# Rotary embedding: the adds of nine tiles on the TensorE, and transfers of 2 MB

## The chip, the cores and the metric

The kernel runs on one core of a Trainium2 chip. The metric is the device time of one execution in microseconds, the median over several runs. A profile is one execution seen by the hardware profiler; its times count from the start of its span.

## The reference

```python
def reference(x, cos, sin):          # x: (8, 2048, 8, 64), cos and sin: (2048, 32), all float32
    x1 = x[..., : x.shape[-1] // 2]
    x2 = x[..., x.shape[-1] // 2 :]
    cos = cos[None, :, None, :]
    sin = sin[None, :, None, :]
    out1 = x1 * cos - x2 * sin
    out2 = x1 * sin + x2 * cos
    return np.concatenate([out1, out2], axis=-1)
```

Every head of 64 numbers is split in two halves of 32. Each output half is one input half times the cosine plus or minus the other half times the sine. The input and the output hold 33.55 MB each, and every byte is read once and written once.

## The kernel before

The sequence of 2048 positions is laid over the 128 partitions, 16 neighbouring positions to a partition. A tile holds four of these 16 for one batch entry: 128 partitions of 2048 floats, which is 1 MB in rows of 8 KB. There are four blocks of positions and eight batch entries, so 32 tiles; the loop runs over the blocks outside and the batch inside.

The two tables are small (0.26 MB each). SBUF holds them in `sin_sb` and `cos_sb`. VectorE builds `ssin` from the sine table (line 58 with the sign turned, line 59 as it is), and copies the cosine table into PSUM as `cos_ps` (line 60). The helper `rep` repeats a table along the heads by an access pattern of step 0, so no repeated table is stored.

The work of a tile is this. GpSimd multiplies the swapped halves of `xt` by `ssin` into `t2`, in two instructions (line 73), one for each half. VectorE multiplies `xt` by `cos_ps` into `t1` in PSUM (line 78), and then adds `t1` and `t2` back into `xt` (line 83). ScalarE issues the store of `xt` (line 84) and computes nothing. All loads of x are issued by SP (line 55), those of the tables by ScalarE (lines 48 and 49).

The buffers are: 20 slots of `xt`, which is 160 KB of each partition, three slots of `t2` in SBUF, and one slot of `t1` in PSUM. The first 20 loads need nothing but a slot; each later load waits for the store of the tile 20 places earlier. The kernel writes no order and no semaphores by hand: the tile framework orders the instructions of each engine and inserts the waits. No engine but VectorE and GpSimd does arithmetic.

Of the kernel before, what the change touches and what calls it, by code (L numbers as in the profile page):

```python
# [2 lines left out]

# [4 lines left out]


@with_exitstack  # L10
def kernel(
    ctx: ExitStack,
    tc: tile.TileContext,
    x: bass.AP,
    cos: bass.AP,
    sin: bass.AP,
    out: bass.AP,
):
    nc = tc.nc
    f32 = mybir.dt.float32  # L20

    B, S, H, D = x.shape
    Dh = D // 2
    P = 128
    HD = H * D
    R = S // P

    SL = 4
    n_blk = R // SL
    FREE = SL * HD  # L30

    xv = x.rearrange("b (q r) h d -> b q (r h d)", q=P)
    ov = out.rearrange("b (q r) h d -> b q (r h d)", q=P)
    cos_src = cos.rearrange("(q r) d -> q r d", q=P)
    sin_src = sin.rearrange("(q r) d -> q r d", q=P)

    const_pool = ctx.enter_context(tc.tile_pool(name="const", bufs=1))
    cps_pool = ctx.enter_context(tc.tile_pool(name="cps", bufs=1, space=bass.MemoryType.PSUM))
    t1_pool = ctx.enter_context(tc.tile_pool(name="t1p", bufs=1, space=bass.MemoryType.PSUM))
    xpool = ctx.enter_context(tc.tile_pool(name="xpool", bufs=20))  # L40
    t2_pool = ctx.enter_context(tc.tile_pool(name="t2p", bufs=3))

    cos_sb = const_pool.tile([P, R, Dh], f32, tag="cb")
    sin_sb = const_pool.tile([P, R, Dh], f32, tag="sb")
    ssin = const_pool.tile([P, R, 2, Dh], f32, tag="ss")
    cos_ps = cps_pool.tile([P, R, Dh], f32, tag="cp")

    nc.scalar.dma_start(out=sin_sb, in_=sin_src)
    nc.scalar.dma_start(out=cos_sb, in_=cos_src)

    tiles = [(b, l) for l in range(n_blk) for b in range(B)]
    xts = []
    for i, (b, l) in enumerate(tiles):
        xt = xpool.tile([P, FREE], f32, tag="xt", name=f"xt{i}")
        nc.sync.dma_start(out=xt, in_=xv[b, :, l * FREE : (l + 1) * FREE])
        xts.append(xt)

    nc.vector.tensor_scalar_mul(ssin[:, :, 0, :], sin_sb, -1.0)  # L58
    nc.vector.tensor_copy(ssin[:, :, 1, :], sin_sb)  # L59
    nc.vector.tensor_copy(cos_ps, cos_sb)  # L60

    def rep(a, n):
        return dataclasses.replace(a, ap=[a.ap[0][:], a.ap[1][:], [0, n], a.ap[-1][:]])

    for i, (b, l) in enumerate(tiles):
        xt = xts[i]
        t1 = t1_pool.tile([P, FREE], f32, tag="t1")
        t2 = t2_pool.tile([P, FREE], f32, tag="t2")

        for u in range(2):  # L70
            dst = t2.rearrange("p (rh u d) -> p rh u d", u=2, d=Dh)[:, :, u, :]
            src = xt.rearrange("p (rh u d) -> p rh u d", u=2, d=Dh)[:, :, 1 - u, :]
            nc.gpsimd.tensor_mul(  # L73
                out=dst.rearrange("p (r h) d -> p r h d", h=H),
                in0=src.rearrange("p (r h) d -> p r h d", h=H),
                in1=rep(ssin[:, l * SL : (l + 1) * SL, u, :], H),
            )
        nc.vector.tensor_mul(  # L78
            out=t1.rearrange("p (r k d) -> p r k d", r=SL, d=Dh),
            in0=xt.rearrange("p (r k d) -> p r k d", r=SL, d=Dh),  # L80
            in1=rep(cos_ps[:, l * SL : (l + 1) * SL, :], 2 * H),
        )
        nc.vector.tensor_add(out=xt, in0=t1, in1=t2)  # L83
        nc.scalar.dma_start(out=ov[b, :, l * FREE : (l + 1) * FREE], in_=xt)


# [1 line left out]
_INS = ['x', 'cos', 'sin']  # L88
_OUTS = [((8, 2048, 8, 64), 'float32')]


# [23 lines left out]
```

## Time and profile before

| | |
|---|---|
| time, median of 8 runs | 168.3 us (168.0 to 168.43) |
| the profiled execution | 168.31 us, of which its span is 166.5 us |
| VectorE busy | 148.2 us, 89% of the span |
| GpSimd busy | 146.3 us, 88% of the span |
| bytes moved | 67.65 MB, on average 406 GB/s over the span |
| loads of x by SP | 32, 1024 KB each, 20.8 us from issue to landing |
| stores by ScalarE | 32, 1024 KB each, 10.8 us from issue to landing |

In the profile DVE is VectorE, POOL is GpSimd, ACT is ScalarE, PE is TensorE and SP is SyncE, which issues loads only; a "q" behind a name means the engine's own queue of issues. A digit in a row of slices is the busy share of one fortieth of the span in tenths. In a line of a group stand the line of the code, the engine, the operation, output and inputs, their shapes and the number of instructions; after the first bar the busy time and the mean duration in ns, and after the second the idle time ahead of the group with what ended it.

### The profile page before, as it was taken

To read this page: it belongs to the slowest core of one execution; us is meant where nothing else is said; L and a number is where in the kernel's file an instruction comes from. 1 tells how busy PE (TensorE), PEld (TensorE's weight loads), DVE (VectorE), ACT (ScalarE), POOL (GpSimd) and SP (SyncE) were. 2 spreads that over 40 slices of the span, in tenths; PEclk is the share of its full clock that TensorE was granted. 3 is DMA by queue.
4 is the path that set the end of the run, shared out by engine and by line. 5 is a ranking of instruction groups with operands and counts; after the bars stand their busy time and mean duration, and the time that the engine had idled before them with its cause. 6 is when DMAs were issued, how large, how long until landed. Compare 5 with 4: busy or idle time off the path is not lost.

```text
span 166.5 us, 381 instructions
## 1 busy us (share of the span) xinstructions
DVE 148.2 (89%) x67; POOL 146.3 (88%) x68
## 2 busy tenths in 40 slices
DVE  0169999999999999999999999999999999999980
POOL 0299999999999999999999999999999999998000
DMA  5999999999999999999999999999999999999656
GB/s 181 427 428 419 378 431 425 425 433 427 427 427 427 427 423 433 425 431 423 425 425 429 425 431 427 427 423 433 429 423 427 429 425 427 429 431 425 272 220 252
DMA packets 9506, 67.65 MB, mean 406 GB/s; under 512 B 1056, under 2 KB 1056, under 8 KB 1312
## 3 DMA queue, kind: packets, MB, share of 16 engines
q10 hardware_dynamic: 4896, 34.08, 48.6%
q1 hardware_dynamic: 4608, 33.56, 48.3%
q14 instruction: 2, 0.02, 0.0%
HBM read 34.08 MB, written 33.55 MB: 406 GB/s over the span
## 4 chain that ended last, share of the span: by engine, by line
POOL 50%; DVE 29%; issue 14%; DMA 4%; DVEq 0%
POOL t L73 50%; DVE xt L83 15%; DVE t L78 14%; DMA sin_sb<-in_sin_dram 4%; DVE ssin L58 0%; DVEq L83 0%
## 5 line engine op out<-in xcount | busy, mean ns | idle before, releaser
L73 POOL TENSOR_TENSOR t<-xt,ssin 128x1024 f32<-128x1024 f32 x64 | 146.1, 2319 | 6.8 <-DVE ssin L58 6.8
L83 DVE TENSOR_TENSOR xt<-t,t 128x2048 f32<-128x2048 f32 x32 | 73.3, 2291 | 3.3
L78 DVE TENSOR_TENSOR t<-xt,cos_ps 128x2048 f32<-128x2048 f32 x32 | 73.5, 2296 | 1.1
L58 DVE TENSOR_SCALAR ssin<-sin_sb 128x512 f32<-128x512 f32 x1 | 0.4, 428 | 6.7 <-DMA sin_sb<-in_sin_dram 6.7
L60 DVE COPY cos_ps<-cos_sb 128x512 f32<-128x512 f32 x1 | 0.7, 695 | 2.4 <-DMA cos_sb<-in_cos_dram 2.4
L59 DVE COPY ssin<-sin_sb 128x512 f32<-128x512 f32 x1 | 0.4, 420 | 0.0
L99 POOL MEMSET const-float32-0.0<- 128x1 f32 x1 | 0.1, 100 | 0.2 <-issue 0.2
L99 POOL MEMSET const-bfloat16-1.0<- 128x1 bf16 x1 | 0.1, 103 | 0.0
L99 POOL MEMSET const-uint8-127<- 128x1 uint8 x1 | 0.1, 103 | 0.0
L99 POOL MEMSET const-float32-1.0<- 128x1 f32 x1 | 0.1, 100 | 0.0
## 6 DMA issues: line engine op xcount, KB each, us to landing
xt<-in_x_dram SPq DMA_DIRECT2D x32, 1024.0 KB, 20.8
out_dram<-xt ACTq DMA_DIRECT2D x32, 1024.0 KB, 10.8
sin_sb<-in_sin_dram ACTq DMA_DIRECT2D x1, 256.0 KB, 5.9
cos_sb<-in_cos_dram ACTq DMA_DIRECT2D x1, 256.0 KB, 8.7
```

The lines of the kernel that those rows point to most:

```text
L58: nc.vector.tensor_scalar_mul(ssin[:, :, 0, :], sin_sb, -1.0)
L59: nc.vector.tensor_copy(ssin[:, :, 1, :], sin_sb)
L60: nc.vector.tensor_copy(cos_ps, cos_sb)
L73: nc.gpsimd.tensor_mul(out=dst.rearrange("p (r h) d -> p r h d", h=H), in0=src.rearrange("p (r h) d -> p r h d", h=H), in1=rep(ssin[:, l * ...
L78: nc.vector.tensor_mul(out=t1.rearrange("p (r k d) -> p r k d", r=SL, d=Dh), in0=xt.rearrange("p (r k d) -> p r k d", r=SL, d=Dh), in1=rep ...
L83: nc.vector.tensor_add(out=xt, in0=t1, in1=t2)
L99: nc = _bacc.Bacc("TRN2", target_bir_lowering=False, num_devices=1)
```

## The change

A pair of tiles now shares one slot `xt`, loaded and stored as 2 MB with rows of 16 KB. Only the first pair is loaded in two halves, and only the last is stored in two. There are nine slots of a pair. The tables' loads move from ScalarE's queue to the head of SP's.

The tiles are of three kinds. An "A" tile is computed as before. A "B" tile leaves its add out of VectorE: VectorE writes `t1` to SBUF (pool `t1s`, three slots), and TensorE multiplies 512 columns of `t1` and of `t2` by an identity matrix, both into the same PSUM bank, so that the bank holds their sum; ScalarE copies the bank to `xt`. A "C" tile leaves GpSimd out too: VectorE multiplies `xt` by the sine into a second `t1s` slot, and TensorE adds that with the halves swapped, with the negative identity where the sign is minus. The kinds stand in a dictionary: tiles 5, 13 and 21 are C, the two tiles behind each are B, the other 23 are A. (The change's short name speaks of ten tiles, and of four C; the last of its steps sets the three groups that the code has.)

The diff, cut to what computes:

```diff
-    xpool = ctx.enter_context(tc.tile_pool(name="xpool", bufs=20))
+    o_pool = ctx.enter_context(tc.tile_pool(name="op", bufs=2, space=PSUM))
+    xpool = ctx.enter_context(tc.tile_pool(name="xpool", bufs=9))
+    t1s_pool = ctx.enter_context(tc.tile_pool(name="t1s", bufs=3))
     t2_pool = ctx.enter_context(tc.tile_pool(name="t2p", bufs=3))
...
-    nc.scalar.dma_start(out=sin_sb, in_=sin_src)
-    nc.scalar.dma_start(out=cos_sb, in_=cos_src)
+    nc.sync.dma_start(out=sin_sb, in_=sin_src)
+    nc.sync.dma_start(out=cos_sb, in_=cos_src)
...
+    for i, (b, l) in enumerate(pairs):
+        xt = xpool.tile([P, PAIR], f32, tag="xt", name=f"xt{i}")
+        for lo, n in [(0, FREE), (FREE, FREE)] if i == 0 else [(0, PAIR)]:
+            nc.sync.dma_start(
+                out=xt[:, lo : lo + n],
+                in_=xv[b, :, l * PAIR + lo : l * PAIR + lo + n],
+            )
...
+    nc.gpsimd.memset(eye, 0.0)
+    nc.gpsimd.affine_select(out=eye, in_=eye,
...
+    nc.scalar.copy(sin_ps, sin_sb)
+    nc.scalar.mul(neye, eye, -1.0)
...
+    kinds = {}
+    for g in (5, 13, 21):
+        kinds |= {g: "C", g + 1: "B", g + 2: "B"}
...
+        if kind == "C":
+            t2 = t1s_pool.tile([P, FREE], f32, tag="t1s", name="t2c")
+        else:
+            t2 = t2_pool.tile([P, FREE], f32, tag="t2")
+        if kind == "A":
+            t1 = t1_pool.tile([P, FREE], f32, tag="t1")
+        else:
+            t1 = t1s_pool.tile([P, FREE], f32, tag="t1s")
...
+        if kind == "C":
+            nc.vector.tensor_mul(
+                out=t2.rearrange("p (r k d) -> p r k d", r=SL, d=Dh),
+                in0=xk,
+                in1=rep(sin_ps[:, r0 : r0 + SL, :], 2 * H),
             )
+        else:
+            for u in range(2):
+                nc.gpsimd.tensor_mul(
...
         nc.vector.tensor_mul(
             out=t1.rearrange("p (r k d) -> p r k d", r=SL, d=Dh),
...
+        if kind == "A":
+            nc.vector.tensor_add(out=xt, in0=t1, in1=t2)
+        elif kind == "B":
+            for j in range(FREE // C):
+                o = o_pool.tile([P, C], f32, tag="o")
+                cs = slice(j * C, (j + 1) * C)
+                nc.tensor.matmul(o, eye, t1[:, cs], start=True, stop=False)
+                nc.tensor.matmul(o, eye, t2[:, cs], start=False, stop=True)
+                nc.scalar.copy(xt[:, cs], o)
+        else:
+            G = C // Dh
+            for u in range(2):
+                for j in range(FREE // 2 // C):
+                    o = o_pool.tile([P, C], f32, tag="o")
+                    gs = slice(j * G, (j + 1) * G)
+                    nc.tensor.matmul(o, eye, t1u[:, gs, u, :], start=True, stop=False)
+                    nc.tensor.matmul(
+                        o, eye if u else neye, t2u[:, gs, 1 - u, :], start=False, stop=True
+                    )
+                    nc.scalar.copy(xu[:, gs, u, :], o.rearrange("p (g d) -> p g d", d=Dh))
...
+        if i == n_tiles - 2:
+            nc.scalar.dma_start(out=ov[b, :, base : base + FREE], in_=xt)
+        elif i == n_tiles - 1:
+            nc.scalar.dma_start(out=ov[b, :, base + FREE : base + PAIR], in_=xt)
+        elif half:
+            nc.scalar.dma_start(out=ov[b, :, base : base + PAIR], in_=pt)
```

## The prediction, made before the changed kernel ran

> **What bounds the kernel now.** I read the page from the top: busy shares, then the 40 slices.
>
> ```profile
> DVE 148.2 (89%) x67; POOL 146.3 (88%) x68
> ...
> DVE  0169999999999999999999999999999999999980
> POOL 0299999999999999999999999999999999998000
> DMA  5999999999999999999999999999999999999656
> GB/s 181 427 428 419 378 431 425 425 433 427 427 427 427 427 423 433 425 431 423 425 425 429 425 431 427 427 423 433 429 423 427 429 425 427 429 431 425 272 220 252
> ```
>
> Three things are full at once. VectorE and GpSimd read 9 from slice 4 on, and the DMA engines move about 427 GB/s from slice 2 to slice 37. Only the last three slices fall to 220 to 272. So there are two nearly equal bounds, and the ends decide which is first. The groups by line give the unit prices:
>
> ```profile
> L73 POOL TENSOR_TENSOR t<-xt,ssin 128x1024 f32<-128x1024 f32 x64 | 146.1, 2319 | 6.8 <-DVE ssin L58 6.8
> L83 DVE TENSOR_TENSOR xt<-t,t 128x2048 f32<-128x2048 f32 x32 | 73.3, 2291 | 3.3
> L78 DVE TENSOR_TENSOR t<-xt,cos_ps 128x2048 f32<-128x2048 f32 x32 | 73.5, 2296 | 1.1
> ```
>
> A tile costs GpSimd 146.1/32 = 4.57 us. VectorE starts a tile every 4.73 us: in the chain below its multiply starts at 152.36 and again at 157.08.
>
> ```profile
> 152.36 2.31 DVE t L78
> ...
> 157.08 2.31 DVE t L78
> ...
> 159.48 2.29 DVE xt L83
> ```
>
> The chain ends in VectorE's last add, at 161.8; the last store follows and the span ends at 166.5, 4.7 us later. The windows show what the transfers did meanwhile:
>
> ```profile
> core 0: us, DVE busy (x) POOL busy (x), PEclk, DMA share, GB/s
> ...
> 156.50:166.50 10.00, 5.14 (x3) 0.00 (x0) 1.00 0.52 213
> 24.00:154.00 130.00, 126.23 (x56) 129.30 (x57) 1.00 1.01 427
> ```
>
> For 130 us the transfers run at a share of 1.01. Only when their backlog is gone do they wait for VectorE: from 156.5 on they move 2.13 MB, which at 427 GB/s takes 5.0 us. With the 1.4 us after the last packet (the slices of transfers in this window end near 165.1) the end would be 156.5 + 5.0 + 1.4 = 162.9. **So a faster VectorE is worth at most 3.6 us; then the transfers are the end.** At the front, the timeline shows:
>
> ```profile
> 7.21 9.27 POOL L73 TENSOR_TENSOR t<-xt,ssin 128x1024 f32<-128x1024 f32 x4 [6.76 <-DVE ssin L58]
> 9.87 0.69 DVE L60 COPY cos_ps<-cos_sb 128x512 f32<-128x512 f32 x1 [2.41 <-DMA cos_sb<-in_cos_dram]
> 10.60 2.30 DVE L78 TENSOR_TENSOR t<-xt,cos_ps 128x2048 f32<-128x2048 f32 x1
> 13.00 2.29 DVE L83 TENSOR_TENSOR xt<-t,t 128x2048 f32<-128x2048 f32 x1
> ```
>
> GpSimd waits for the sine table until 7.2, VectorE for the cosine table until 9.9; the tables share the engines with x.
>
> **What the Trainium skill says.** "FP8 and Floating Point Precision", TensorE Precision Notes: true FP32 takes four passes through the array. "TensorE: Matmul & The Clock Gate", Back-to-back issue gap: N/1.2 ns per matmul cold, N/2.4 + 2.5 ns warm; its Part 1 says that the clock starts at half and rises after some 3.4 us of sustained work. The trace of before has no matmul, so neither is confirmed. "GPSIMD Engine Reference", 1. Specifications: GpSimd contends with VectorE instructions with two SBUF inputs. Here every VectorE operation on a tile has one PSUM input (`cos_ps` or `t1`), GpSimd is at 129.3 of 130 us, and the change keeps that form (`sin_ps`, `cos_ps`), so I keep 4.57 us.
>
> **The change part by part.**
>
> *Tables first, on SP.* 0.52 MB of tables, then 1.05 MB of x in one queue. The tables' 2 KB packets took 84 ns (85 of them are 11.2% of 16 engines in the window from 1 to 5 us), so they need 1.4 us; the first packets move at about 1.7, half a pair takes 2.5 us, and some 0.8 us passes until it has landed: 6.4. GpSimd starts near 6.5 (0.7 earlier), VectorE's first multiply too, and its first add follows GpSimd at 6.5 + 4.6 = 11.1 against 13.0. Gain 1.9 us of VectorE. The identity and its negative are made meanwhile by engines that are idle until 6.5: cost nothing; a bound of 1 us if GpSimd's select is slow. SP issues 19 DMAs instead of 32 and ScalarE 17 instead of 34, at 0.33 us each; neither queue was what the transfers waited for.
>
> *2 MB transfers.* A packet of 8 KB took 309 ns (588 packets with 523 of data, 101.4% of ten us of 16 engines), one of 2 KB 84 ns: a fixed 9 ns and 27.3 GB/s. A 16 KB packet would take 609 ns where two take 618: 1.5% of 158 us, 2.3 us. The other bound is nothing, if rows are cut. I take half, 1.1 us: the floor is 161.8. Nine slots of 2 MB hold 18 MB against 20; the first store waits for two tiles, but loads fill that time.
>
> *VectorE.* The code marks nine tiles, not the ten of the change's title. Six "B" lose the add (6 x 2.36 = 14.2 us); three "C" have two multiplies, as dear as before (2.291 and 2.296 us to SBUF and to PSUM show that the target is free). *GpSimd* loses three tiles: 3 x 4.57 = 13.7 us.
>
> *TensorE and ScalarE.* Each of the nine tiles needs eight matmuls of 512 columns. Four passes at 2.4 GHz make 0.86 us each, at 1.2 GHz 1.71 us (both from the pages' prices). With about 4 us of cold start a group of three takes 8.9 + 6.9 + 6.9 = 22.7 us; cold throughout 41. The four evacuations of a tile by ScalarE cost 186 + 0.833 x 512 = 0.61 us each by "ScalarE: Activation LUTs", What ACT_TABLE_LOAD costs; two output banks cover that behind 1.7 us of matmuls.
>
> *The waits that come in.* First, the second B of a group takes a `t1s` slot that C holds until its last matmul. Queued behind it on VectorE are all later A tiles. Second, each B keeps its `t2` until TensorE has read it, so GpSimd has one of three slots meanwhile. Walk a group, from VectorE's start of tile 5 at 31.7. C's multiplies end at 36.4, TensorE works C until 45.4, B 6 until 52.3, B 7 until 59.2. B 6's multiply ends at 38.8. The order of VectorE's stream is left to the tile framework, which can put ready work of tile 8 ahead of the blocked B 7; nothing in the trace of before shows such a choice. **I take it that it does so.** Then tile 8 is multiplied at 38.8, added by 45.4 (GpSimd has it at 43.1), B 7 is multiplied until 47.8, tile 9 ends at 52.4 (GpSimd 45.4 to 50.0, having waited 2.3), tile 10 at 59.2 (GpSimd 52.3 to 56.9, again 2.3), 11 at 63.9, 12 at 68.6. Eight tiles take 36.9 us against 37.8 before. The last add: 31.7 + 3 x 36.9 + 3 x 4.73 = 156.6, the store to 161.3. ScalarE issues the stores and waits in its stream for TensorE; those of pairs 2 and 3 come late, while loads have slots to fill the engines.
>
> *Sum.* Compute ends at 161.3, the transfers at 161.8; I add 0.7 for gaps at the hand-over from loads to stores: span 162.5. The profiled execution took 168.31 for a span of 166.5, 1.8 around it, and lies on the median of 168.3. **Forecast 164.3 us**, 2.4% less.
>
> **The rivals.**
>
> *1. TensorE becomes the bound through the slots (slower).* If VectorE's stream stays in program order, B 7's multiply stands from 38.8 to 45.4 with everything behind it. Tile 8 then ends at 52.6, tile 9 waits for GpSimd, which got its slot at 52.3, until 59.3, tile 10 (slot at 59.2) until 66.2, 12 until 75.7: 44.0 us a group, that is 21.3 plus TensorE's 22.7. The end is 31.7 + 132 + 14.2 + 4.7 = 182.6, so 184.4 us. It is slower once TensorE needs over 17.3 us a group (31.7 + 3p + 14.2 + 4.7 = 166.5 gives p = 38.6), 0.72 us a matmul. For it: three slots and four passes. Against it: work of tile 8 is ready. A stream partly in that order gives values between, from 169.
>
> *2. The clock stays low.* 13.7 us a tile, 41.1 a group. With reordering TensorE sets the period: near 175 us; in program order near 239. For it: TensorE is idle between groups. Against it: a group is longer than the rise takes.
>
> *3. The transfers lose what the engines gain.* Large transfers on nine slots leave a gap while stores wait for a group; 4 to 5 us of it bring 167.5 to 169. Against it: by 97 us, the end of the second group, full engines have moved 95.5 us x 427 GB/s = 40.8 MB, some nineteen transfers of a pair; with seven pairs stored twelve are loaded, and sixteen (nine slots and the seven set free) could be.
>
> *4. Faster matmuls or none of these waits:* compute ends near 157, and the transfers alone set 160.5 to 162.9: 162.3 to 164.7.
>
> **How the numbers follow.** My forecast with rival 4 has 0.58, its own range 162.4 to 167.5; rival 1 0.22 (169 to 186); rival 2 0.12; rival 3 0.08, half of it within 0.2% of before, which is about what a measurement of this kernel can tell from no change. Faster: 0.58 + 0.02 = 0.60. Same: 0.05. Slower: 0.35. The range of 162.4 to 182 leaves out the upper half of rival 1, most of it on the 239 side of rival 2, and 0.03 below.
>
> **What the profile would show.** Right: DMA near 427 to 433 GB/s until the last slices, the last add near 157, matmul groups of about 22 us, VectorE near 138 us and GpSimd near 133 us busy. The first add near 11. Rival 1: VectorE's line of the `t1s` multiply waiting some 6.6 us for TensorE three times, and GpSimd waiting for TensorE. Rival 2: matmuls of 1.7 us throughout. Rival 3: slices of DMA under 8 with VectorE busy. A compute end after 158 would make the forecast wrong.

## The result, and the profile after

The changed kernel takes **177.04 us** (median of 11 runs, 175.84 to 177.92) against 168.29 us in runs of the kernel before beside it: a ratio of 1.052, with a 95% interval of 1.0504 to 1.0536. The forecast was 164.3 us, and the chance given to slower was 0.35. The time lies inside the range, but it moved the other way. The profiled execution has a span of 175.0 us. A run more than 1.5% above the fastest of its kernel counts as slow; every ratio here compares fast runs alone, and only the first run with five `t2` slots, further down, has slow ones (8 of its 20, the profiled one among them).

From the page of the changed kernel, its busy times and slices:

```profile
PE 80.9 (46%) x144; PEld 32.8 (19%) x144; DVE 132.6 (76%) x61; ACT 22.5 (13%) x39; POOL 133.9 (77%) x64
...
DVE  1158999994499949995994949992994679999920
...
POOL 1089999999409499999909499999846899999400
...
DMA  4999999999999999999999999999999960918995
GB/s 154 303 427 438 423 371 427 427 423 446 434 427 427 423 446 434 427 427 419 446 438 423 429 416 449 434 427 421 419 448 431 408 258 0 419 60 360 420 419 240
...
POOL 59%; issue 17%; DVE 14%; DMA 4%; SPq 0%; DVEq 0%; POOLq 0%
```

The work did leave the two engines, as forecast: VectorE fell from 148.2 to 132.6 us and GpSimd from 146.3 to 133.9. What came in is the holes. Three times, every eight tiles, GpSimd's row falls to 4 or below with VectorE's low beside it, and the transfers run dry twice near the end, in slices 33 and 34 and again in 36. The last line is the chain of work that ended last.

The lines of the changed kernel are these: 123 is GpSimd's multiply, 128 VectorE's multiply by the cosine and 134 its add; 116 is VectorE's multiply by the sine in a C tile. Lines 139 and 140 are the matmuls of a B tile and 141 the copies of its banks by ScalarE; 148, 149 and 152 are the same of a C tile; 160 is the store of a pair. The waits of the same kernel, with the waiting group, what it waited for, the total, the number and the longest:

```profile
ACT xt L141 <- DVE xt L134: 67.4, 7, 10.7
...
PE o L139 <- ACT xt L141: 37.9, 6, 7.5
...
POOL t L123 <- DVE xt L134: 21.4, 6, 7.1
...
DVE xt L134 <- POOL t L123: 14.7, 7, 2.4
DVE t L128 <- PE o L148: 10.1, 3, 4.7
POOL t L123 <- DMA xt<-in_x_dram: 7.9, 1, 7.9
```

GpSimd has the largest part of the chain, 59%: it starts at 9.2, is busy for 133.2 us on tiles and waits 21.4 us for VectorE's adds, together 163.8. Its last multiply ends at 163.95. From 141.1 us on the chain runs through VectorE's last multiplies and adds, with GpSimd about 1 us ahead of it; the last add ends at 167.2. One group shows how the waits arise (the timeline from 38 to 61 us; start, duration, engine and line, and the idle time ahead in brackets):

```profile
38.96 2.27 DVE L128 TENSOR_TENSOR t<-xt,cos_ps 128x2048 f32<-128x2048 f32 x1
45.94 4.49 DVE L128 TENSOR_TENSOR t<-xt,cos_ps 128x2048 f32<-128x2048 f32 x2 [4.70 <-PE o L148]
...
46.59 1.02 PE L139 MATMUL o<-t,eye 128*128 128x512 f32 x2
...
50.53 2.29 DVE L134 TENSOR_TENSOR xt<-t,t 128x2048 f32<-128x2048 f32 x1
...
52.91 4.63 POOL L123 TENSOR_TENSOR t<-xt,ssin 128x1024 f32<-128x1024 f32 x2 [7.12 <-DVE xt L134]
...
53.46 1.02 PE L139 MATMUL o<-t,eye 128*128 128x512 f32 x2
...
57.56 2.29 DVE L134 TENSOR_TENSOR xt<-t,t 128x2048 f32<-128x2048 f32 x1 [0.34 <-POOL t L123]
...
59.93 2.34 POOL L123 TENSOR_TENSOR t<-xt,ssin 128x1024 f32<-128x1024 f32 x1 [2.40 <-DVE xt L134]
```

At 38.96 VectorE multiplies the first B tile of the group. VectorE's next line is the second B together with tile 8 ("x2"), and it stands 4.70 us until TensorE has finished with C's operands. So tile 8's add ends only at 52.8, and GpSimd, whose slot for tile 9 is the one that this add sets free, stands 7.12 us. For tile 10 it waits again, for the add of tile 9, although TensorE had left the first B, and with it a slot, near 53.5, where the second B's matmuls begin; so tile 10 was given the slot of tile 9 and not that one.

### The profile page after: what moved, and what is told of

It reads as the page before. It is cut to its first block, busy times and chain, and to the rows that moved or that the text cites. A ratio compares the mean times of both kernels' runs of the same rounds, so it can differ in the third digit from the quotient of the medians.

```text
span 175.0 us, 632 instructions
## 1 busy us (share of the span) xinstructions
PE 80.9 (46%) x144; PEld 32.8 (19%) x144; DVE 132.6 (76%) x61; ACT 22.5 (13%) x39; POOL 133.9 (77%) x64
## 4 chain that ended last, share of the span: by engine, by line
POOL 59%; issue 17%; DVE 14%; DMA 4%; SPq 0%; DVEq 0%; POOLq 0%
POOL t L123 59%; DVE xt L134 8%; DVE t L128 7%; DMA xt<-in_x_dram 4%; SPq L57 0%; SPq L56 0%; DVEq L134 0%; POOLq L123 0%
## 5 line engine op out<-in xcount | busy, mean ns | idle before, releaser
L123 POOL TENSOR_TENSOR t<-xt,ssin 128x1024 f32<-128x1024 f32 x58 | 133.2, 2332 | 29.5 <-DVE xt L134 21.4
L128 DVE TENSOR_TENSOR t<-xt,cos_ps 128x2048 f32<-128x2048 f32 x32 | 72.8, 2291 | 15.0 <-PE o L148 10.1
L134 DVE TENSOR_TENSOR xt<-t,t 128x2048 f32<-128x2048 f32 x23 | 52.7, 2290 | 16.0 <-POOL t L123 14.7
L139 PE MATMUL o<-t,eye 128*128 128x512 f32 x48 | 33.1, 778 | 37.9 <-ACT xt L141 37.9
L148 PE MATMUL o<-t,eye 128*128 128x512 f32 x24 | 15.4, 728 | 37.0 <-DVE t L128 37.0
L140 PE MATMUL o<-t,eye 128*128 128x512 f32 x48 | 30.2, 716 | 0.0
L141 ACT COPY xt<-o 128x512 f32<-128x512 f32 x24 | 13.4, 588 | 83.2 <-DVE xt L134 67.4
L139 PEld LDWEIGHTS o<-t,eye 128*128 128x128 f32 x48 | 11.0, 245 | 53.7 <-ACT xt L141 42.8
L140 PEld LDWEIGHTS o<-t,eye 128*128 128x128 f32 x48 | 11.4, 236 | 16.1 <-issue 16.1
L152 ACT COPY xt<-o 128x512 f32<-128x512 f32 x12 | 7.0, 586 | 51.2 <-PE o L149 51.2
L148 PEld LDWEIGHTS o<-t,eye 128*128 128x128 f32 x24 | 5.1, 228 | 44.7 <-POOL t L123 37.0
L149 PE MATMUL o<-t2c,neye 128*128 128x512 f32 x12 | 7.4, 703 | 0.0
L116 DVE TENSOR_TENSOR t2c<-xt,sin_ps 128x2048 f32<-128x2048 f32 x3 | 6.8, 2280 | 0.0
L149 PE MATMUL o<-t2c,eye 128*128 128x512 f32 x12 | 6.1, 592 | 0.0
L149 PEld LDWEIGHTS o<-t2c,neye 128*128 128x128 f32 x12 | 3.1, 257 | 4.5 <-issue 4.5
L149 PEld LDWEIGHTS o<-t2c,eye 128*128 128x128 f32 x12 | 2.3, 190 | 2.9 <-issue 2.9
## 6 DMA issues: line engine op xcount, KB each, us to landing
out_dram<-xt ACTq DMA_DIRECT2D x15, 2048.0 KB, 14.2
```

The lines of the kernel that those rows point to most:

```text
L116: nc.vector.tensor_mul(out=t2.rearrange("p (r k d) -> p r k d", r=SL, d=Dh), in0=xk, in1=rep(sin_ps[:, r0 : r0 + SL, :], 2 * H),)
L123: nc.gpsimd.tensor_mul(out=t2u[:, :, u, :].rearrange("p (r h) d -> p r h d", h=H), in0=xu[:, :, 1 - u, :].rearrange("p (r h) d -> p r h d" ...
L128: nc.vector.tensor_mul(out=t1.rearrange("p (r k d) -> p r k d", r=SL, d=Dh), in0=xk, in1=rep(cos_ps[:, r0 : r0 + SL, :], 2 * H),)
L139: nc.tensor.matmul(o, eye, t1[:, cs], start=True, stop=False)
L140: nc.tensor.matmul(o, eye, t2[:, cs], start=False, stop=True)
L141: nc.scalar.copy(xt[:, cs], o)
```

## The experiments

Two theories stood against each other. **A**: ScalarE's stream has stores of later pairs between the evacuations of B tiles; such a store waits for a VectorE add, TensorE then waits for ScalarE (the largest numbers of the list), and the slots stay taken. **B**: VectorE stands for a `t1s` slot, its add is late, and GpSimd waits for the `t2` slot that this add sets free.

### ScalarE's stream in program order

```diff
-                nc.scalar.copy(xt[:, cs], o)
+                tc.keep_in_program_order(nc.scalar.copy(xt[:, cs], o))
```

and the same around the other evacuation and the three stores. The call keeps an instruction at the program's own place in its engine's stream; below, these edits are called the pins.

> The changed kernel with ScalarE's stream pinned to program order: a store no longer stands ahead of evacuations that are ready. Theory A (ScalarE's stream blocks TensorE, whose late end holds the slots): TensorE's 37.9 us of waits for ScalarE go, and with them most of the loss, so about 166 us. Theory B (VectorE stands for a t1s slot behind each C tile, its add is late, and GpSimd waits for the t2 slot that this add sets free): GpSimd's 21.4 us of waits stay; only the store of the eleventh pair, which left at 163.0, leaves earlier and shortens the tail by up to 3 us, so 174 to 176 us.

Measured: 177.64 us, ratio 1.0558 (1.0528 to 1.0587). From its waits:

```profile
PE o L148 <- DVE t L128: 71.3, 3, 37.7
...
POOL t L123 <- DVE xt L134: 24.8, 6, 7.3
DVE xt L134 <- POOL t L123: 14.8, 7, 2.4
DVE t L128 <- PE o L148: 13.0, 3, 4.9
```

TensorE no longer waits for ScalarE's copies at all, 37.9 us of waits are gone, and the time is no shorter. Theory A falls as the cause of the loss. B's waits stayed, and GpSimd's grew by 3.4 us.

The time is above the 174 to 176 us expected under B as well, because two effects cancel. The tail from the last add to the end did shrink, from 7.8 us (167.2 to 175.0) to 5.0 (170.9 to 175.9). But TensorE, no longer held up, is done with a group early, stands idle for 15.8 and 17.8 us, and starts the second and third groups cold, at half its pace (0.85 us between matmul records instead of 0.43). The second group's C tile and the matmul behind it, first in the changed kernel, then here:

```profile
76.27 1.20 PE L148 MATMUL o<-t,eye 128*128 128x512 f32 x2
...
83.32 1.02 PE L139 MATMUL o<-t,eye 128*128 128x512 f32 x2
```

```profile
77.22 2.05 PE L148 MATMUL o<-t,eye 128*128 128x512 f32 x2 [15.80 <-DVE t L128]
...
86.05 1.02 PE L139 MATMUL o<-t,eye 128*128 128x512 f32 x2
```

C takes 7.05 us where a late second B tile reaches up to it, and 8.83 us behind the idle stretch. The three C tiles together take 27.7 us instead of 24.8, and VectorE's waits for them grow by as much, from 10.1 to 13.0 us.

### Which slots

The control with eight pair slots, then five `t1s` slots, then five `t2` slots (the latter two with eight pair slots):

```diff
-    xpool = ctx.enter_context(tc.tile_pool(name="xpool", bufs=9))
+    xpool = ctx.enter_context(tc.tile_pool(name="xpool", bufs=8))
-    t1s_pool = ctx.enter_context(tc.tile_pool(name="t1s", bufs=3))
+    t1s_pool = ctx.enter_context(tc.tile_pool(name="t1s", bufs=5))      # second of the three
-    t2_pool = ctx.enter_context(tc.tile_pool(name="t2p", bufs=3))
+    t2_pool = ctx.enter_context(tc.tile_pool(name="t2p", bufs=5))       # third of the three
```

> A control: eight instead of nine pair slots of x, which makes room for the slots of the next two runs. Theories A and B both expect no change within 0.5% (177 us), since compute, not the loads, sets the end; a theory that the loads are short of slots expects over 179 us.

Measured: 176.99 us. A pair slot fewer changes nothing.

> Eight pair slots, five t1s slots instead of three: the second B of a group need not wait for C's matmuls. Theory A: no gain, 177 us. Theory B: VectorE's 10.1 us of waits for TensorE go, GpSimd's first wait of each group falls from 7.1, 3.9 and 3.1 to about 2.4, together some 7 us less, so 169 to 171 us, unless the tail of late stores grows.

Measured: 197.58 us, 20.6 us more than with eight pair slots alone.

```profile
ACT xt L152 <- DVE xt L134: 42.6, 2, 25.8
POOL t L123 <- DVE xt L134: 40.4, 13, 11.6
```

VectorE's waits for TensorE did go, but GpSimd's waits for adds rose to 40.4 us in 13 pieces, and a store stood for up to 25.8 us ahead of evacuations of a C tile in ScalarE's stream. The forecast of this run was wrong.

> Eight pair slots, five t2 slots instead of three: GpSimd can run ahead while TensorE holds the slots of two B tiles. Theory A: no gain, 177 us. Theory B: GpSimd's 21.4 us of waits go although VectorE's 10.1 us stay; GpSimd ends near 143 us and VectorE becomes the end: from its first add at 13.9 some 132.6 - 4 us of work and 10.1 us of waits give a last add near 154 to 158 and a time of 164 to 168 us.

Measured: 168.3 us as the median of 20 runs scattered from 166.2 to 170.8; the twelve behind the ratio of 0.997 (0.9949 to 0.9991) have a median of 167.6. The profile is of a run of 169.3 us. From its waits:

```profile
DVE t L128 <- PE o L148: 12.4, 3, 4.3
POOL t L123 <- DMA xt<-in_x_dram: 7.8, 1, 7.8
POOL t L123 <- DVE xt L134: 7.1, 2, 5.2
```

VectorE still stands 12.4 us for TensorE, but GpSimd waits 7.1 us instead of 21.4, and 9.4 us of time are back (167.6 against 176.99). So the shortage of `t2` slots, not VectorE's standing by itself, carries most of the loss. In this profile the last add ends at 159.7 and the span at 167.6; the store of the pair with the last two B tiles leaves at 155.4, behind later pairs.

### ScalarE's order again, now with the slots

> Eight pair slots, five t2 slots, and ScalarE's stream in program order. In the run with five t2 slots alone the last add ended at 159.7, but the store of the eleventh pair left only at 155.4 behind other stores and the end came 7.9 us after the last add. If the late store in ScalarE's stream makes that tail, it falls to about 5 us and the time to 164 to 166.5 us, below the kernel before. If the tail has another cause, 168 us.

The edit is the two above together:

```diff
-    t2_pool = ctx.enter_context(tc.tile_pool(name="t2p", bufs=3))
+    t2_pool = ctx.enter_context(tc.tile_pool(name="t2p", bufs=5))      # eight pair slots
-            nc.scalar.dma_start(out=ov[b, :, base : base + PAIR], in_=pt)
+            tc.keep_in_program_order(nc.scalar.dma_start(out=ov[b, :, base : base + PAIR], in_=pt))
```

Measured: 166.74 us, ratio 0.9917 (0.9895 to 0.994), just above the expected range. From its waits:

```profile
POOL t L123 <- DVE xt L134: 6.1, 3, 4.0
```

Against the pinned run with three `t2` slots (177.64 us) the time is 10.9 us shorter, and GpSimd's waits fall from 24.8 to 6.1 us. The two runs differ in the `t2` slots and in one pair slot, which alone changed nothing, so the slots' part is seen a second time.

The pins themselves bring 0.9 us here (167.6 to 166.7). The last add ends at 158.7 and the span at 164.5, 5.7 us later, where the 169.3 us run without pins had 7.9. With three `t2` slots the pins shortened this tail too, by 2.8 us. That the late store is what the 0.9 us come from fits, but it is not shown: no profile of one of the twelve lower runs without pins was kept.

The same pins with five `t1s` slots:

```diff
-    t1s_pool = ctx.enter_context(tc.tile_pool(name="t1s", bufs=3))
+    t1s_pool = ctx.enter_context(tc.tile_pool(name="t1s", bufs=5))     # eight pair slots
```

> Eight pair slots, five t1s slots, and ScalarE's stream in program order. With five t1s slots alone the time was 197.6 us; there ScalarE held the evacuations of a C tile behind a store for up to 25.8 us. If that order was the cause, it is gone here: VectorE does not stand for C's matmuls, GpSimd keeps its waits of about 2.4 us, two in each group, and the time is 168 to 172 us. If more t1s slots hurt in another way, over 185 us.

Measured: 191.63 us. ScalarE's order explains only some 6 of the 20 us that five `t1s` slots cost, so the first of the two expected cases did not come. The timeline behind its second group shows where the rest goes:

```profile
86.41 2.29 DVE L116 TENSOR_TENSOR t2c<-xt,sin_ps 128x2048 f32<-128x2048 f32 x1 [6.97 <-DMA xt<-in_x_dram]
...
90.98 4.63 POOL L123 TENSOR_TENSOR t<-xt,ssin 128x1024 f32<-128x1024 f32 x2 [9.01 <-DVE xt L134]
95.65 2.29 DVE L134 TENSOR_TENSOR xt<-t,t 128x2048 f32<-128x2048 f32 x1 [2.42 <-POOL t L123]
...
98.02 4.60 POOL L123 TENSOR_TENSOR t<-xt,ssin 128x1024 f32<-128x1024 f32 x2 [2.40 <-DVE xt L134]
102.65 2.29 DVE L134 TENSOR_TENSOR xt<-t,t 128x2048 f32<-128x2048 f32 x1 [2.38 <-POOL t L123]
```

C's sine multiply stands in VectorE's stream ahead of an add that is ready, and waits 6.97 us for its load. After that, GpSimd and VectorE share one `t2` slot: GpSimd 4.6 us, then the add 2.3 us, and each stands while the other works. A tile takes 7.0 us (95.65 to 102.65) instead of 4.73. GpSimd waits for adds 14 times in this run, 40.3 us in all. Why this lasts for more tiles with five `t1s` slots than with three was not tried and stays open.

### The second B moved back

The slots of the change, ScalarE's stream in program order, and one line:

```diff
-        kinds |= {g: "C", g + 1: "B", g + 2: "B"}
+        kinds |= {g: "C", g + 1: "B", g + 3: "B"}
```

> The slots of the change (9, 3, 3), ScalarE's stream in program order, and the second B tile of each group moved one place back, so that an A tile stands between the two B tiles: the order that the prediction took for granted. If VectorE's standing at the second B is what makes GpSimd's first wait long, VectorE's waits for TensorE fall from 13 us to under 4, GpSimd's waits from 24.8 to about 15, and the time to 168 to 171 us. If GpSimd's waits come from the three t2 slots whatever VectorE does, 176 to 178 us.

Measured: 172.46 us, ratio 1.0248 (1.023 to 1.0267), 5.2 us less than the pinned run with adjacent B tiles (177.64).

```profile
POOL t L123 <- DVE xt L134: 19.0, 6, 7.0
DVE xt L134 <- POOL t L123: 18.4, 11, 2.5
...
DVE t2c L116 <- DMA xt<-in_x_dram: 5.0, 1, 5.0
```

VectorE waits for TensorE nowhere, and GpSimd's waits fall by 5.8 us. Five of the six are now 2.4 us, as the prediction's walk had all six; the sixth, 7.0 us, stands behind a wait of VectorE for a load, 5.0 us at a C multiply again. So the order "tile 8 before the second B" is worth about 5.2 us here. The time fell short of the expected 168 to 171 by that wait for a load.

### The transfers and the start alone

```diff
-    for g in (5, 13, 21):
+    for g in ():
```

> The transfers of the change and its tables ahead on SP, but no tile on TensorE: all 32 are of kind A. With the first add at 13.9 and 4.73 us a tile the last add ends at 162.7 and the store 4.7 to 6.6 later; span 167.4 to 169.3, time 169 to 171 us: the large transfers alone cost 1 to 3 us through the late first half pair. If they cost nothing, 168 us; if they gain by their rows, 165 us.

Measured: 169.49 us, ratio 1.0065 (1.005 to 1.008); the second run also moves the tables back:

```diff
-    nc.sync.dma_start(out=sin_sb, in_=sin_src)
-    nc.sync.dma_start(out=cos_sb, in_=cos_src)
+    nc.scalar.dma_start(out=sin_sb, in_=sin_src)
+    nc.scalar.dma_start(out=cos_sb, in_=cos_src)
```

> As the run with all tiles of kind A, but the two tables are loaded by ScalarE again, so that the first half pair is the first in SP's queue. That run's GpSimd waited until 9.4 us for its first half pair, against 7.2 before. If the single queue with the tables at its head makes the first half pair late, GpSimd starts near 7, and the time falls from 169.5 by about 2 us to 167 to 168. If the 16 KB rows behind it make it late, GpSimd still starts after 9 and the time stays at 169.5.

Measured: 168.21 us, ratio 1.0008 (1.0 to 1.0017). GpSimd's first instruction in the first run and in the second:

```profile
9.43 11.43 POOL L123 TENSOR_TENSOR t<-xt,ssin 128x1024 f32<-128x1024 f32 x5 [8.12 <-DMA xt<-in_x_dram]
```

```profile
6.97 13.83 POOL L123 TENSOR_TENSOR t<-xt,ssin 128x1024 f32<-128x1024 f32 x6 [5.67 <-DVE ssin L80]
```

With the tables ahead in SP's queue the first half pair lands after 9 us; with the tables in another queue, GpSimd starts 2.5 us earlier and about 1 us of the time returns (1.3 by the medians, 1.0 by the ratios). The transfers of 2 MB by themselves cost nothing that shows (ratio 1.0008).

### What is left when the waits are gone

All three have the pins, eight pair slots and the tables on ScalarE:

```diff
-    nc.sync.dma_start(out=sin_sb, in_=sin_src)
+    nc.scalar.dma_start(out=sin_sb, in_=sin_src)
...
-    t2_pool = ctx.enter_context(tc.tile_pool(name="t2p", bufs=3))
+    t2_pool = ctx.enter_context(tc.tile_pool(name="t2p", bufs=5))      # third run: 4, and four t1s slots
...
-        kinds |= {g: "C", g + 1: "B", g + 2: "B"}
+        kinds |= {g: "C", g + 1: "B", g + 3: "B"}                      # second and third run only
```

> The run of 166.7 us (ScalarE's stream in program order, five t2 slots, eight pair slots) with the tables loaded by ScalarE. If the start is still worth what it is to the kernel without TensorE, 1.5 to 2.5 us are won: 164 to 165.5 us. If the transfers already set the end of that run, at most 0.5 us: 166.2 to 166.8.

> The same, with the second B tile of each group moved one place back, which takes VectorE's waits for TensorE (12.6 us there) away. If VectorE sets the end, it comes 4 us or more earlier, until the transfers hold it: 161.5 to 164 us. If the transfers do, as in the run before, no change beyond 0.5 us.

> The same again with four t1s slots and four t2 slots instead of three and five. If GpSimd's sharing of one t2 slot with VectorE is what costs, four slots leave some of it: 1 to 4 us more than the run with five. If t2 is no longer the scarce one, equal within 0.5 us.

Measured: 164.90, 164.89 and 164.93 us; the ratios are 0.9817 (0.9804 to 0.9831), 0.9814 (0.9801 to 0.9828) and 0.9818 (0.9804 to 0.9831). All three are 1.8% below the kernel before, with intervals well clear of 1, and below the changed kernel. The first gained 1.8 us by the start (166.74 to 164.90), as its larger expectation said; the second and third gained nothing further. The windows of the first of them and of the second, in that order (time, busy time of PE, PEld, DVE, ACT and POOL, clock, DMA share, GB/s):

```profile
30.00:130.00 100.00, 67.68 (x141) 29.21 (x142) 85.59 (x39) 19.93 (x34) 92.85 (x41) 0.85 1.01 431
130.00:150.00 20.00, 1.88 (x5) 0.57 (x3) 19.36 (x9) 1.17 (x2) 17.32 (x8) 0.66 1.00 429
150.00:157.00 7.00, 0.00 (x0) 0.00 (x0) 6.66 (x4) 0.00 (x0) 0.00 (x0) 0.50 0.98 418
```

```profile
30.00:130.00 100.00, 68.46 (x144) 29.41 (x144) 91.04 (x41) 20.42 (x35) 94.26 (x42) 0.90 1.01 431
130.00:150.00 20.00, 0.26 (x1) 0.00 (x0) 19.17 (x9) 0.59 (x1) 15.96 (x7) 0.64 1.01 432
150.00:157.00 7.00, 0.00 (x0) 0.00 (x0) 1.48 (x1) 0.00 (x0) 0.00 (x0) 0.50 0.98 420
```

In the second, VectorE is through at 151.5 (1.48 us of work after 150), in the first at 157.5, and the spans are 163.2 and 163.0. Six us of VectorE are worth nothing here: the transfers run full until 157 in both and set the end. The third run did not separate the slots, for the same reason.

## Why the prediction was wrong

**What held.** The floor: the prediction put it at 162.9 us of span, or 161.8 with half of the rows' gain; in the last three runs, with the waits gone and the tables in their old place, the span is 163.0 to 163.2, and their 164.9 us are near the forecast of 164.3. The rows: 16 KB rows moved 431 to 432 GB/s in mid-run against 427, about 1%, between the bounds of nothing and 1.5%. TensorE's price: a warm B tile took 6.87 us (46.59 to 53.46) against 6.9, and the first C tile, started cold, 9.6 us against 8.9. "FP8 and Floating Point Precision", TensorE Precision Notes, and "TensorE: Matmul & The Clock Gate", Back-to-back issue gap, agree with the trace: eight matmuls of 512 columns in 6.87 us are 0.86 us each, the price of four passes at the full clock. The matmuls kept the slow spacing for 5.2 us in the first group (36.99 to 42.24) and 3.5 us in the pinned run's second (77.22 to 80.76), around the prediction's 4. ScalarE's copies took 0.59 us against 0.61. GpSimd's pace did not suffer (133.2 us for 29 tiles, 4.59 each), so "GPSIMD Engine Reference", 1. Specifications, has no contention to show here. The work taken from GpSimd and VectorE came about as counted.

**The step that failed** is the one marked "I take it that it does so", that tile 8 overtakes the blocked second B tile in VectorE's stream. It does not: both multiplies stand behind C's matmuls, by 4.70, 2.1 and 3.3 us in the three groups. GpSimd's waits are then 21.4 us instead of the forecast's six of 2.3 us, 13.8 together: 7.6 us more. That is the mechanism of rival 1 in part of its size, and its range of 169 to 186 us holds the result; its other sign, GpSimd waiting for TensorE, did not come, for every wait of GpSimd in the groups is for an add. The run with the second B moved back takes this order away, and 5.2 us with it.

**Two terms were mis-sized.** The first half pair was to land at 6.4 and landed at 9.1, which starts GpSimd 2.7 us late. The tables ahead in the queue are the cause (the run with the tables on ScalarE's queue), but how is open. The sum priced the transfers at the full rate; the changed kernel has 309 GB/s from 4.5 to 9 us, yet the run with five `t2` slots and pins has 428 GB/s there, and its GpSimd starts at 9.2 all the same:

```profile
4.50:9.00 4.50, 0.00 (x0) 0.00 (x0) 0.53 (x1) 0.00 (x0) 0.00 (x0) 1.00 1.02 428
```

The tail from the last add to the end was to be 5.9 us by the sum and is 7.8. The store of the pair with the last two B tiles left at 163.0, because ScalarE's evacuations stood behind stores; with ScalarE's stream pinned the tail is 5.0. What the prediction said of the late stores of pairs 2 and 3, that loads fill the engines meanwhile, holds for the first two groups and not for the third, behind which no loads are left.

The sum closes to 0.3 us. The last add came at 167.2 instead of 156.6: 7.6 us for GpSimd's waits, 2.7 for its start, and 0.3 that no term covers. The tail adds 1.9. Together these are 12.5 us, from the forecast span of 162.5 to 175.0. Two figures of the prediction do not follow from its own prices, without bearing on the sign: tile 5 would start at 32.3 (11.1 + 4 x 4.73 + 2.3) and not at 31.7, and VectorE would be busy for 134.0 us (148.2 - 14.2) and not near 138; it was 132.6.

The six waits of 2.3 us that the forecast itself counted came from the shortage of `t2` slots as well, and were not followed up. Five `t2` slots removed two thirds of GpSimd's waits at once, whatever VectorE's order.

**Rivals 2 and 3.** TensorE's clock did rise within each group (mean 0.836 over the span), so rival 2 fell. The dry slices of rival 3 exist, but at the end only, where the compute is late.

## What to carry to other kernels

When work is moved to an engine that is slower per tile, count how long it holds the buffers of the engines that feed it: two of three slots held for 7 us and more turn two overlapped engines into two that take turns, at 7.0 us a tile instead of 4.7. Look at the waits on the chain, not at the longest entry of the list: taking away 37.9 us of TensorE's waits did not shorten the time, while the 21.4 us of GpSimd's held it. And an engine that is freed to finish early may start its next stretch cold (8.83 us for a C tile here instead of 7.05). An order left to a framework is a case of its own in a prediction: price both orders, and give the range the weight of the worse one.

## What the runs showed of the hardware

A load of 1 MB that follows two tables of 2 KB rows in one queue landed 7.4 us after its issue; as the first of its queue, with the tables in another, such a load landed after 5.5 us. The rate of the transfers does not explain it: it landed as late in a run with 428 GB/s in that stretch as in one with 309. A float32 matmul of 512 columns appears in the profile as two matmul records of 0.43 us spacing each when warm, 0.85 when cold (144 records for 72 matmuls). After 15.8 us of idleness a C tile took 8.83 us, with TensorE busy up to its start 7.05. And more slots of one buffer can cost 20 us: with five `t1s` slots the time rose from 177 to 197.6 us, by waits that lay in other engines.
